# Row means of a 64 MB tensor: rows regrouped into three parts, one load ahead of the opening barrier

## Chip, cores, metric

One core of one Trainium2 chip. The metric is device time in microseconds (us) of one execution. "Ratio" is the figure that the measuring program gives for one kernel's fast runs against the other's in the same rounds, so it is not quite the ratio of the medians quoted beside it, nor of the plain means; the bracket after it is a 95% interval. "Step" or "pitch" is the distance in memory between the places where two neighbouring partitions begin to read.

## The reference

```python
x = np.random.randn(32, 512, 1024).astype(np.float32)     # 64 MiB
def reference(x, divisor):                                  # divisor = 1024.0
    return (np.sum(x, axis=-1) / divisor).astype(np.float32)
```

That is 16,384 rows of 4 KiB, 128 rows for each of the 128 partitions.

## The kernel before

It gives each partition 120 consecutive rows in a main part and 8 in a last part. Loads of 14 rows per partition go through three buffers. VectorE sums most rows, ScalarE a few of the later ones. The last row of each partition comes in three pieces and is closed by one accumulating operation, so that little is left to do after the last byte arrives.

```python
L = 8
M = J - L                                   # J = 128
x_main = bass.AP(tensor=x.tensor, offset=0, ap=[[M * D, P], [D, M], [1, D]])
x_last = bass.AP(tensor=x.tensor, offset=P * M * D, ap=[[L * D, P], [D, L], [1, D]])
# ... o_main, o_last likewise
main = [(14, 0)] * 6 + [(14, 4), (14, 6), (8, 4)]     # (rows, of them on ScalarE)
last = [(4, 2), (2, 1)]
# ... pools: bulk (3 buffers), one, psum
res = one.tile([P, M], F32, name="res")
fin = one.tile([P, L], F32, name="fin")               # q, r: the same size

for rows, on_act in main:
    t = bulk.tile([P, 14, D], F32, name="t")
    load(t[:, :rows, :], x_main[:, j : j + rows, :])
    sums(res[:, j : j + rows], t, rows, on_act)       # reduce_sum on VectorE, activation on ScalarE
    j += rows
# ... last: t4, t2 in tiles of their own; then one row, then three pieces pa, pb, pc of the last row
nc.gpsimd.tensor_scalar_mul(out=res, in0=res, scalar1=scale)
tc.keep_in_program_order(nc.sync.dma_start(out=o_main, in_=res))
# ... sums of pa, pb into two columns behind pc; means of the other last rows
nc.vector.tensor_scalar(
    out=scaled, in0=pc, scalar1=scale, scalar2=0.0, op0=MULT, op1=ADD, accum_out=fin[:, L - 1 :]
)
tc.keep_in_program_order(nc.sync.dma_start(out=o_last, in_=fin))
```

After the build, `start_loads_at_once` moves every load that waits for nothing (three of them) ahead of the opening barrier of all engines.

## Time and profile before

| | before |
|---|---|
| time, median of the first three runs | 161.70 us (161.69 to 161.78) |
| span in the profile | 160.1 us |
| VectorE / ScalarE busy | 75% / 13% |
| DMA engines under packets | 97.8% of the span |
| first load landed, first reduction starts | 19.58 us |

The page reads as a stream of loads with sums hidden behind it; the prediction shows the lines. Two lines of the DMA view complete them (columns: transfer, queue, operation, number, KB each, median us from issue to landing). They tell how deep the queue is: the last piece of the last row waits 35.7 us behind other loads, the store of 120 means 5.2 us.

```profile
pc<-in_x_dram SPq DMA_DIRECT2D x1, 160.0 KB, 35.7
...
out_dram<-res SPq DMA_DIRECT2D x1, 60.0 KB, 5.2
```

### The profile page before, as it was taken

To read this page: it belongs to the slowest core of one execution; us is meant where nothing else is said; L and a number is where in the kernel's file an instruction comes from. 1 tells how busy PE (TensorE), PEld (TensorE's weight loads), DVE (VectorE), ACT (ScalarE), POOL (GpSimd) and SP (SyncE) were. 2 spreads that over 40 slices of the span, in tenths; PEclk is the share of its full clock that TensorE was granted. 3 is DMA by queue.
4 is the path that set the end of the run, shared out by engine and by line. 5 is a ranking of instruction groups with operands and counts; after the bars stand their busy time and mean duration, and the time that the engine had idled before them with its cause. 6 is when DMAs were issued, how large, how long until landed. Compare 5 with 4: busy or idle time off the path is not lost.

```text
span 160.1 us, 138 instructions
## 1 busy us (share of the span) xinstructions
DVE 119.9 (75%) x16; ACT 20.7 (13%) x39; POOL 0.8 (1%) x6
## 2 busy tenths in 40 slices
DVE  0000199968998699959995999599987990497985
ACT  3000000000000000000000000000007300491973
POOL 0000000000000000000000000000000000000010
DMA  8899999998899999998899999999799999999993
GB/s 301 387 458 458 458 458 458 458 430 358 358 458 458 458 458 458 458 458 387 358 401 458 458 458 458 458 458 430 315 401 458 458 458 458 393 393 405 415 402 104
DMA packets 2448, 67.18 MB, mean 419 GB/s; under 512 B 528, under 2 KB 912, under 8 KB 1040
## 3 DMA queue, kind: packets, MB, share of 16 engines
q1 hardware_dynamic: 2448, 67.18, 97.8%
HBM read 67.11 MB, written 0.07 MB: 419 GB/s over the span
## 4 chain that ended last, share of the span: by engine, by line
DMA 67%; DVE 29%; another core or an unknown queue 1%; SPq 1%; issue 0%; DVEq 0%
DMA t<-in_x_dram 45%; DVE res L153 28%; DMA row<-in_x_dram 22%; SPq L142 1%; DVE q L173 1%; DVE scaled L195 0%; DVE pc L190 0%; DVE fin L191 0%; DVEq L195 0%; DVEq L229 0%
## 5 line engine op out<-in xcount | busy, mean ns | idle before, releaser
L153 DVE TENSOR_REDUCE res<-t 128x14 f32<-128x14336 f32 (+3 forms) x9 | 114.4, 12716 | 37.9 <-DMA t<-in_x_dram 37.9
L147 ACT ACTIVATE junk<-t 128x1024 f32<-128x1024 f32 x17 | 17.2, 1011 | 135.2 <-DMA t<-in_x_dram 135.2
L153 DVE TENSOR_REDUCE q<-t 128x2 f32<-128x2048 f32 (+1 forms) x2 | 3.5, 1752 | 0.7 <-DMA t<-in_x_dram 0.7
L147 ACT ACTIVATION_READ_ACCUMULATOR junk<-t 128x1 f32 x17 | 3.2, 186 | 0.0
L147 ACT ACT_TABLE_LOAD x1 | 1.3, 1283 | 1.7 <-PEq L215 1.7
L186 POOL TENSOR_SCALAR res<-res 128x120 f32<-128x120 f32 x1 | 0.5, 512 | 150.5 <-DVE res L153 150.5
L173 DVE TENSOR_REDUCE q<-row 128x1 f32<-128x768 f32 x1 | 1.0, 953 | 0.1
L195 DVE TENSOR_SCALAR_CACHE_REDUCE scaled<-pc 128x322 f32<-128x322 f32 x1 | 0.5, 490 | 0.1
L147 ACT ACTIVATE junk<-pa 128x448 f32<-128x448 f32 x1 | 0.5, 547 | 0.1
L190 DVE TENSOR_REDUCE pc<-pb 128x1 f32<-128x256 f32 x1 | 0.4, 412 | 0.0
L147 ACT ACTIVATE junk<-row 128x256 f32<-128x256 f32 x1 | 0.4, 387 | 0.1
L191 DVE SCALAR_TENSOR_TENSOR fin<-q,r 128x7 f32<-128x7 f32 x1 | 0.2, 167 | 0.0
L147 ACT ACTIVATION_READ_ACCUMULATOR junk<-row 128x1 f32 x1 | 0.2, 187 | 0.0
L147 ACT ACTIVATION_READ_ACCUMULATOR junk<-pa 128x1 f32 x1 | 0.2, 186 | 0.0
L139 POOL MEMSET r<- 128x8 f32 x1 | 0.1, 104 | 1.3 <-POOLq L215 1.3
L215 POOL MEMSET const-bfloat16-1.0<- 128x1 bf16 x1 | 0.1, 101 | 0.0
L215 POOL MEMSET const-uint8-127<- 128x1 uint8 x1 | 0.1, 101 | 0.0
L215 POOL MEMSET const-float32-0.0<- 128x1 f32 x1 | 0.1, 99 | 0.2 <-issue 0.2
L215 POOL MEMSET const-float32-1.0<- 128x1 f32 x1 | 0.1, 98 | 0.0
L195 DVE DVE_READ_ACCUMULATOR scaled<-pc 128x1 f32 x1 | 0.1, 82 | 0.0
## 6 DMA issues: line engine op xcount, KB each, us to landing
t<-in_x_dram SPq DMA_DIRECT2D x8, 7168.0 KB, 35.7
t<-in_x_dram SPq DMA_DIRECT2D x1, 4096.0 KB, 28.5
t<-in_x_dram SPq DMA_DIRECT2D x1, 2048.0 KB, 33.0
t<-in_x_dram SPq DMA_DIRECT2D x1, 1024.0 KB, 35.0
row<-in_x_dram SPq DMA_DIRECT2D x1, 512.0 KB, 35.8
pa<-in_x_dram SPq DMA_DIRECT2D x1, 224.0 KB, 36.0
pc<-in_x_dram SPq DMA_DIRECT2D x1, 160.0 KB, 35.7
pb<-in_x_dram SPq DMA_DIRECT2D x1, 128.0 KB, 35.9
```

The lines of the kernel that those rows point to most:

```text
L139: nc.gpsimd.memset(r, 0.0)
L142: tc.keep_in_program_order(nc.sync.dma_start(out=dst, in_=src))
L147: nc.scalar.activation(junk[:, :n], src, COPY, scale=by, accum_out=dst)
L153: nc.vector.reduce_sum(out=dst[:, :d], in_=t[:, :d, :], axis=AX)
L173: nc.vector.reduce_sum(out=q[:, j : j + 1], in_=row[:, :c], axis=AX)
L186: nc.gpsimd.tensor_scalar_mul(out=res, in0=res, scalar1=scale)
L190: nc.vector.reduce_sum(out=pc[:, D - b + 1 :], in_=pb, axis=AX)
L191: nc.vector.scalar_tensor_tensor(out=fin[:, : L - 1], in0=q[:, : L - 1], scalar=scale, in1=r[:, : L - 1], op0=MULT, op1=ADD)
L195: nc.vector.tensor_scalar(out=scaled, in0=pc, scalar1=scale, scalar2=0.0, op0=MULT, op1=ADD, accum_out=fin[:, L - 1 :])
L215: nc = _bacc.Bacc("TRN2", target_bir_lowering=False, num_devices=1)
```

## The change

Its intent: write back a first half of the means while loads still run, keep less ahead of the barrier, and leave 16 instead of 8 rows to the last part, whose very last row is closed by the same accumulating step. Cut to its core:

```diff
-def start_loads_at_once(nc):            # moves all loads that wait for nothing
+def start_first_load_at_once(nc):       # moves the first load alone
...
-    L = 8
-    M = J - L
-    x_main = bass.AP(tensor=x.tensor, offset=0, ap=[[M * D, P], [D, M], [1, D]])
-    x_last = bass.AP(tensor=x.tensor, offset=P * M * D, ap=[[L * D, P], [D, L], [1, D]])
+    B, L = 56, 16
+    def part(t, first, n, width):
+        cols = [[width, n], [1, width]] if width > 1 else [[1, n]]
+        return bass.AP(tensor=t.tensor, offset=first * P * width, ap=[[n * width, P]] + cols)
+    x_part = [part(x, 0, B, D), part(x, B, B, D), part(x, 2 * B, L, D)]
...
-    main = [(14, 0)] * 6 + [(14, 4), (14, 6), (8, 4)]
-    last = [(4, 2), (2, 1)]
+    main = [[(14, 0)] * 4, [(14, 0)] * 2 + [(14, 4), (14, 6)]]
+    last = [(8, 4), (4, 2), (2, 1)]     # the load of 8 uses a bulk buffer
-    res = one.tile([P, M], F32, name="res")
+    res = [one.tile([P, B], F32, name=f"res{k}") for k in range(2)]
...
+    def means_out(k):
+        nc.gpsimd.tensor_scalar_mul(out=res[k], in0=res[k], scalar1=scale)
+        tc.keep_in_program_order(nc.sync.dma_start(out=o_part[k], in_=res[k]))
...
+            if k == 1 and j == B:       # right after the eighth bulk load is issued
+                means_out(0)
...                                      # means_out(1) where the one store of means was
```

More of the change, by code (lines that the diff above doesn't have):

```diff
@@ L15 @@
 SP = mybir.EngineType.SP
-def start_loads_at_once(nc):
+def start_first_load_at_once(nc):
     first, body = nc.main_func.blocks[0], nc.main_func.blocks[1]
-    loads = []
-    for i in body.instructions:
-        if i.engine == SP:
-            if type(i).__name__ != "InstDMACopy" or (i.sync_info and i.sync_info.on_wait):
-                break
-            loads.append(i)
-    names = {i.name for i in loads}
-    assert names
-    body.instructions = [i for i in body.instructions if i.name not in names]
+    load = next(i for i in body.instructions if i.engine == SP)
+    assert type(load).__name__ == "InstDMACopy" and not load.sync_info.on_wait
+    body.instructions = [i for i in body.instructions if i.name != load.name]
     at = next(
@@ L34, in start_loads_at_once @@
     )
-    first.instructions = first.instructions[:at] + loads + first.instructions[at:]
+    first.instructions = first.instructions[:at] + [load] + first.instructions[at:]
 def with_sync(i, on_wait=None, on_update=None):
@@ L108 @@
     landed = nc.alloc_semaphore("landed")
-    nc.at_finalize(start_loads_at_once)
+    nc.at_finalize(start_first_load_at_once)
     nc.at_finalize(latest_wait_first)
@@ L117 @@
     assert J * P == N
-    L = 8
-    M = J - L
-    x_main = bass.AP(tensor=x.tensor, offset=0, ap=[[M * D, P], [D, M], [1, D]])
-    x_last = bass.AP(tensor=x.tensor, offset=P * M * D, ap=[[L * D, P], [D, L], [1, D]])
-    o_main = bass.AP(tensor=out.tensor, offset=0, ap=[[M, P], [1, M]])
-    o_last = bass.AP(tensor=out.tensor, offset=P * M, ap=[[L, P], [1, L]])
-    main = [(14, 0)] * 6 + [(14, 4), (14, 6), (8, 4)]
-    last = [(4, 2), (2, 1)]
-    assert sum(n for n, _ in main) == M and sum(n for n, _ in last) == L - 2
+    B, L = 56, 16
+    assert 2 * B + L == J
+    def part(t, first, n, width):
+        cols = [[width, n], [1, width]] if width > 1 else [[1, n]]
+        return bass.AP(tensor=t.tensor, offset=first * P * width, ap=[[n * width, P]] + cols)
+    x_part = [part(x, 0, B, D), part(x, B, B, D), part(x, 2 * B, L, D)]
+    o_part = [part(out, 0, B, 1), part(out, B, B, 1), part(out, 2 * B, L, 1)]
+    main = [[(14, 0)] * 4, [(14, 0)] * 2 + [(14, 4), (14, 6)]]
+    last = [(8, 4), (4, 2), (2, 1)]
+    assert all(sum(n for n, _ in m) == B for m in main) and sum(n for n, _ in last) == L - 2
     bulk = ctx.enter_context(tc.tile_pool(name="bulk", bufs=3))
@@ L153, in sums @@
         nc.vector.reduce_sum(out=dst[:, :d], in_=t[:, :d, :], axis=AX)
-    j = 0
-    for rows, on_act in main:
-        t = bulk.tile([P, 14, D], F32, name="t")
-        load(t[:, :rows, :], x_main[:, j : j + rows, :])
-        sums(res[:, j : j + rows], t, rows, on_act)
-        j += rows
+    def means_out(k):
+        nc.gpsimd.tensor_scalar_mul(out=res[k], in0=res[k], scalar1=scale)
+        tc.keep_in_program_order(nc.sync.dma_start(out=o_part[k], in_=res[k]))
+    for k in range(2):
+        j = 0
+        for rows, on_act in main[k]:
+            t = bulk.tile([P, 14, D], F32, name="t")
+            load(t, x_part[k][:, j : j + rows, :])
+            sums(res[k][:, j : j + rows], t, rows, on_act)
+            j += rows
+            if k == 1 and j == B:
+                means_out(0)
     j = 0
     for rows, on_act in last:
-        t = one.tile([P, rows, D], F32, name=f"t{rows}")
-        load(t, x_last[:, j : j + rows, :])
+        if rows == 8:
+            t = bulk.tile([P, 14, D], F32, name="t")[:, :8, :]
+        else:
+            t = one.tile([P, rows, D], F32, name=f"t{rows}")
+        load(t, x_part[2][:, j : j + rows, :])
         sums(q[:, j : j + rows], t, rows, on_act)
@@ L170 @@
     row = one.tile([P, D], F32, name="row")
-    load(row, x_last[:, j, :])
+    load(row, x_part[2][:, j, :])
     act_sum(r[:, j : j + 1], row[:, c:], by=scale)
@@ L180 @@
     pc = one.tile([P, D - b + 2], F32, name="pc")
-    load(pa, x_last[:, L - 1, :a])
-    load(pb, x_last[:, L - 1, a:b])
-    load(pc[:, : D - b], x_last[:, L - 1, b:])
-    nc.gpsimd.tensor_scalar_mul(out=res, in0=res, scalar1=scale)
-    tc.keep_in_program_order(nc.sync.dma_start(out=o_main, in_=res))
+    load(pa, x_part[2][:, L - 1, :a])
+    load(pb, x_part[2][:, L - 1, a:b])
+    load(pc[:, : D - b], x_part[2][:, L - 1, b:])
+    means_out(1)
     act_sum(pc[:, D - b : D - b + 1], pa)
@@ L197 @@
     )
-    tc.keep_in_program_order(nc.sync.dma_start(out=o_last, in_=fin))
+    tc.keep_in_program_order(nc.sync.dma_start(out=o_part[2], in_=fin))
 _INS = ['x', 'divisor']
```

## The prediction

> **What bounds the kernel now.** I looked first at the busy shares and the rows of slices on the profile page, then at the DMA section, then at the timeline for the cadence of the stages, and last at the chain of work that ended last for the tail.
>
> The page of the kernel before, its first lines, the DMA row of the slices and the queue line:
>
> ```profile
> span 160.1 us, 138 instructions
> ...
> DVE 119.9 (75%) x16; ACT 20.7 (13%) x39; POOL 0.8 (1%) x6
> ...
> DMA  8899999998899999998899999999799999999993
> ...
> q1 hardware_dynamic: 2448, 67.18, 97.8%
> HBM read 67.11 MB, written 0.07 MB: 419 GB/s over the span
> ```
>
> No compute engine is over 75%, while packets occupy the sixteen DMA engines for 97.8% of the span. The row shows no hole between the first two slices and the last. So this is a stream of loads with reductions hidden behind it. The timeline says the same with its cadence (columns: start, duration, engine, line, operation, and in brackets the idle time before it and what ended that):
>
> ```profile
> 19.58 15.09 DVE L153 TENSOR_REDUCE res<-t 128x14 f32<-128x14336 f32 x1 [19.58 <-DMA t<-in_x_dram]
> 36.52 15.09 DVE L153 TENSOR_REDUCE res<-t 128x14 f32<-128x14336 f32 x1 [1.86 <-DMA t<-in_x_dram]
> 53.47 15.09 DVE L153 TENSOR_REDUCE res<-t 128x14 f32<-128x14336 f32 x1 [1.86 <-DMA t<-in_x_dram]
> ```
>
> Each reduction takes 15.09 us, then VectorE idles 1.86 us for the next load. A load of 14 rows per partition is 128 x 57,344 bytes = 7.34 MB; one per 16.95 us is 433 GB/s. The trace's records of single packets agree: in steady state one engine moves 57,344 bytes in 2.116 us, 27.1 bytes per ns, and sixteen of them 433.6 GB/s. The slices of 315 or 358 GB/s on the page are not slow stretches: a slice is 4 us, a packet 2.1 us, and a packet's bytes fall into one slice. The packets themselves do not get longer there.
>
> Against this floor, 4.194 MB per engine at 27.1 bytes per ns are 154.8 us. The first packets start 1.02 us into the span and last 2.99 and 2.79 us on average in the first two groups of eight (steady state 2.12), about 0.8 us lost once. Small packets near the end cost some tenths more. That reaches the last load's last packet at 157.4 us. There is almost nothing left in the stream to win.
>
> The last stretch, from the chain of work that ended last (start, duration, what):
>
> ```profile
> 120.72 35.84 DMA row<-in_x_dram
> 156.56 0.02 issue
> 156.58 0.96 DVE q L173
> 157.55 0.02 issue
> 157.57 0.17 DVE fin L191
> 157.74 0.34 DVE pc L190
> 158.08 0.04 DVEq L195
> 158.11 0.07 issue
> 158.18 0.49 DVE scaled L195
> ```
>
> The load of the last but one row lands at 156.56 us; three VectorE operations follow back to back until 158.08; then the accumulating operation on the last row closes. The last piece of that row landed, by its semaphore, at 157.91 us, so it is about 0.15 us off the path. The final store is issued at 158.71 us. The tail follows the arrival of the loads, one to one.
>
> [...] The kernel before has a pitch of 480 KiB in its main part and 32 KiB in its last, both without loss here.[...]
>
> **The change part by part.** The instruction lists of the two kernels show the same eight loads of 14 rows, one of 8, of 4, of 2, of 1, and the three pieces of the last row, the same splits between VectorE and ScalarE, and the same three bulk buffers. Bytes read are the same.
>
> *Only the first load ahead of the barrier.* Loads two and three now come after the opening barrier, which before opened at 1.74 us (ACT table load and a memset start there); an issue is 0.4 us. Without two issues ahead of it the barrier should open near 0.9 to 1.0 us. The second load needs to be in the queue only when the first runs dry, near 18.5 us. It has some 17 us to spare, so this costs nothing. The first load leaves at the same place, so it gains nothing either. ScalarE and GpSimd start 0.8 us earlier and wait anyway.
>
> *The first 112 rows in two blocks of 56; the 8-row load joins the last part.* The pitch per partition goes from 480 KiB to 224 KiB, and for the last 16 rows to 64 KiB.[...] I put zero, with some risk, since no trace so far shows 224 or 64.
>
> *A store in the middle of the stream.* The first 56 means leave after the eighth bulk load has been issued (that is at VectorE's end of the fifth reduction, 87.36 + 15.09 = 102.45 us; the means were ready at 85.5 us). [...]its packets run between the last bulk load and the 8-row load, near 137.7 us, and everything behind moves by their length. Packets: 128 of 224 bytes, 8 per engine. Interpolating between the measured 32 bytes at 9 ns and 480 bytes at 26 ns gives 9 + 192/448 x 17 = 16 ns; eight are 0.13 us, with one more semaphore write (9 ns) 0.14 us. This is on the path: **+0.14 us**.
>
> *The second store* has 224 bytes instead of 480 and is issued after its reduction of 8 rows (about 147 us) rather than at 152.93. It still stands behind all loads, and ends 8 x 10 ns = 0.08 us sooner relative to them. Before, it landed at 158.13 us while the accumulating operation ran until 158.67, so its end was hidden: 0.
>
> *Waits of the queue.* There are eight completion semaphores in turn, and one more transfer shifts the turn: the last piece of the last row now waits for the eighth bulk load (138.2 us) instead of the seventh (121.2). Ahead of it are still the 8-row load and all the small ones, until about 157 us. Nothing runs dry: 0.
>
> *The tail.* The operation that makes the means of the last part has 15 columns instead of 7; at the reduction's 15,086 ns / 14,336 = 1.05 ns per column: **+0.01 us**, in the chain. The final store has 64 bytes a row instead of 32: 8 packets x about 1.2 ns = **+0.01 us**. The accumulating last operation is in both kernels, 322 columns wide.
>
> Sum: +0.14 + 0.01 + 0.01 = +0.16 us on 161.7, so 161.86; I round to 161.9.
>
> **The rivals.** *The new pitch slows the reads.* For it: 64 KiB is a power of two[...]; the last part's packets are short. Against it: a power of two (32 KiB) was used in the last part before, and its 16,384-byte packets ran at 26.6 bytes per ns against 27.1. If the last part lost 10% of its 20 us, that would be 163.9; if the main parts lost 1%, 163.2. I give something like this one chance in ten, most of it smaller.
>
> *The store in the stream makes a bubble.* A write to HBM between reads might let the DMA engines run dry[...]: the first packets of the program show about 0.8 us for starting cold. That would make 162.6. Against it: semaphore writes between loads cause no visible gap, and at the tail of before the store's packets follow the loads without one.
>
> *The opening gets faster.* Three issues in a row may have slowed the first packets; with one issue they may run at 2.1 us instead of 2.9. That would win at most 0.8 us: 161.0. Against it: all sixteen engines show the long first packet whatever its start (1.02 to 1.83 us)[...]. The opposite, the second load late, would need a barrier of over 15 us.
>
> **Range and chances.** Three timed runs of before lie within 0.09 us, so noise is small. From the opening I allow -0.3 us, from bubble and pitch +0.6: 161.5 to 162.5. Two per cent are 3.2 us. To be that much faster the stream would have to beat its wall of 154.8 us plus start and tail, which I cannot see: 0.01. To be that much slower the pitch would have to cost 2%: 0.02. Within 2%: 0.97.
>
> **What would show it right or wrong.** Right: a span near 160.3 us, DMA occupied 97 to 98%, VectorE's first reduction at 19.6 us and the following ones 16.95 apart with 1.86 us of idle time; ACT's table load near 0.9 us; the 8-row load landing near 148.0 instead of 147.87; the last piece of the last row with about 20 us from issue to landing instead of 35.7; the chain ending in the same operations. Wrong: reductions further apart than 16.95 us (pitch of the main parts), a later arrival of only the loads behind the store (bubble, if it is one step at 138 us; pitch of the last part, if it grows with each load), or a first reduction well before 19.5 us (opening). A VectorE that no longer idles between reductions would mean that I misread the bound altogether.

The sum of this forecast came to +0.16 us on 161.7, that is 161.86. Two things stand as estimates from packets of before: the wall of 154.8 us (27.1 bytes per ns in steady state) and the zero for the row blocks (27.1 at a pitch of 480 KiB, 26.6 at 32 KiB). That the store's packets keep their place among the loads, which the +0.14 us takes for granted, agrees with the trace of before: the packets of 57,344 bytes begin at 1.02 us, those of 32,768 at 137.17, of 16,384 at 146.87, and of the store of 480 bytes at 156.86 while loads run until 157.40, in the order of issue. The same trace has 16 semaphore updates for each of its 17 transfers, on eight semaphores in turn but for the last store, and 272 packets of 4 bytes of 9 ns, taken for their writes.

## The result, and the profile after

Changed: 161.91 us median of 4 runs (161.71 to 162.08). Before, in the same rounds: 161.69 (161.69 to 161.78). Ratio 1.0012 [0.9994, 1.0029]: no difference by 2%, nor one clear of zero. The time lies within 0.01 us of the rounded forecast, 161.9, and 0.05 us over its sum, 161.86.

The page of the changed kernel, the same four rows as before:

```profile
span 160.5 us, 140 instructions
...
DVE 119.9 (75%) x16; ACT 20.7 (13%) x39; POOL 1.0 (1%) x7
...
DMA  9899999999989999999888999999988999999991
...
q1 hardware_dynamic: 2592, 67.18, 97.5%
```

VectorE does the same work; there are 144 packets more (128 of the additional store, 16 of 4 bytes, the semaphore writes: 288 in the span for 18 transfers, 272 for 17 before) for the same bytes read. The timeline of the changed kernel (columns as in the prediction):

```profile
0.79 1.28 ACT L145 ACT_TABLE_LOAD   x1 [0.79 <-PEq L222]
...
20.06 15.09 DVE L151 TENSOR_REDUCE res<-t 128x14 f32<-128x14336 f32 x1 [20.06 <-DMA t<-in_x_dram]
36.98 15.09 DVE L151 TENSOR_REDUCE res<-t 128x14 f32<-128x14336 f32 x1 [1.83 <-DMA t<-in_x_dram]
53.92 15.09 DVE L151 TENSOR_REDUCE res<-t 128x14 f32<-128x14336 f32 x1 [1.86 <-DMA t<-in_x_dram]
```

The barrier opens at 0.79 us instead of 1.74, about as foreseen (0.9 to 1.0). The cadence is unchanged: 16.92 and 16.94 us. But the first reduction starts at 20.06 us, not at 19.58 as before, and that was not foreseen. The end of the chain of waits (start, duration, what):

```profile
155.69 1.22 DVE q L151
156.91 0.01 issue
156.93 0.96 DVE q L181
157.89 0.02 issue
157.91 0.17 DVE fin L198
...
158.53 0.49 DVE scaled L202
```

The same operations close, but the reduction of the last but one row starts only 0.35 us later than before (156.93 against 156.58), although the stream started 0.48 us later and a store stands in it. So something near the end got faster. The DMA view:

```profile
pc<-in_x_dram SPq DMA_DIRECT2D x1, 160.0 KB, 19.6
...
out_dram<-res SPq DMA_DIRECT2D x2, 28.0 KB, 23.0
```

The last piece is issued later (it waits for the eighth bulk load) and still lands in its turn; the median of the two stores, 23 us, is that of one in the middle of the queue and one at its end.

So the total was right, and the profile already says that its terms were not: a late start, a faster tail. The records of single packets say where. They do not name the engine, but sixteen packets run side by side (exactly sixteen in about 145 of the 150 us from 5 to 155 us, never fewer), which I take for one on each of the sixteen engines. The times at which these first sixteen packets of 57,344 bytes end:

```
                 first   second ...  15th    last of 16
before           3.86    3.92        4.35    4.38 us
changed          3.75    3.80        4.29    4.88 us
```

One engine alone is late by about half a microsecond, and it stays so: the last packet of the first load ends at 19.68 us, the one before it at 19.08, and the load counts as landed at 20.04 us (before: 19.17, 19.15 and 19.56). The loads that follow keep their distance of 16.9 us, so the late start stays in the whole stream: the last packet of the eight bulk loads ends at 138.15 us against 137.64 before. From 5 to 155 us the records show at least sixteen packets under way at every moment in the changed kernel, also around the store: nothing is lost in the stream itself.

### The profile page after: what moved, and what is told of

The parts are those of the page before. It is cut to its first block, busy times and chain, and to the rows that moved or that the text cites. A ratio compares the mean times of both kernels' runs of the same rounds, so it can differ in the third digit from the quotient of the medians.

```text
span 160.5 us, 140 instructions
## 1 busy us (share of the span) xinstructions
DVE 119.9 (75%) x16; ACT 20.7 (13%) x39; POOL 1.0 (1%) x7
## 4 chain that ended last, share of the span: by engine, by line
DMA 67%; DVE 30%; another core or an unknown queue 1%; SPq 0%; issue 0%; DVEq 0%
DMA t<-in_x_dram 67%; DVE res L151 28%; DVE q L151 1%; DVE q L181 1%; SPq L140 0%; DVE scaled L202 0%; DVE pc L197 0%; DVE fin L198 0%; DVEq L202 0%; DVEq L236 0%
## 5 line engine op out<-in xcount | busy, mean ns | idle before, releaser
L151 DVE TENSOR_REDUCE res<-t 128x14 f32<-128x14336 f32 (+2 forms) x8 | 110.0, 13753 | 37.3 <-DMA t<-in_x_dram 37.3
L151 DVE TENSOR_REDUCE q<-t 128x4 f32<-128x4096 f32 (+2 forms) x3 | 7.9, 2642 | 1.6 <-DMA t<-in_x_dram 1.5
L154 POOL TENSOR_SCALAR res<-res 128x56 f32<-128x56 f32 x2 | 0.7, 352 | 146.2 <-DVE res L151 146.2
## 6 DMA issues: line engine op xcount, KB each, us to landing
pc<-in_x_dram SPq DMA_DIRECT2D x1, 160.0 KB, 19.6
```

The costliest lines, as they stand in the source:

```text
L151: nc.vector.reduce_sum(out=dst[:, :d], in_=t[:, :d, :], axis=AX)
L154: nc.gpsimd.tensor_scalar_mul(out=res[k], in0=res[k], scalar1=scale)
```

## The experiments

Twelve runs, five rounds each, four to a chip. The timed figures of before on the three chips were 161.73, 161.69 and 161.76 us (nine runs each). For every run I also read two figures from its profile: the start of the first reduction ("first"), and the time of that same execution less this start ("rest"). The rest takes the chance of the start out of the comparison.

| kernel | step between partitions, first load | loads ahead | stores in mid-stream | median us | ratio to before | first us | rest us |
|---|---|---|---|---|---|---|---|
| before | 480 KiB | 3 | 0 | 161.69 | | 19.58 | 142.12 |
| changed | 224 | 1 | 1 | 161.91 | 1.0012 | 20.06 | 141.99 |
| r0 | 224 | 1 | 1 | 161.97 | 1.0015 | 19.82 | 141.99 |
| r1 | 480 | 1 | 0 | 161.80 | 1.0008 | 19.63 | 142.09 |
| r2 | 224 | 3 | 1 | 161.82 | 1.0010 | 19.94 | 141.98 |
| r3 | 448 | 3 | 0 | 161.35 | 0.9976 | 19.46 | 141.97 |
| r4 | 224 | 3 | 0 | 161.83 | 1.0009 | 20.09 | 141.91 |
| r5 | 224 | 3 | 2 | 162.15 | 1.0021 | 20.25 | 142.10 |
| r6 | 448 | 3 | 1 | 161.41 | 0.9985 | 19.23 | 142.01 |
| r7 | 448 | 1 | 0 | 161.37 | 0.9988 | 19.36 | 142.41 |
| r8 (= r3) | 448 | 3 | 0 | 161.37 | 0.9979 | 19.38 | 141.92 |
| r9 (= r7) | 448 | 1 | 0 | 161.49 | 0.9983 | 19.46 | 141.92 |
| r10 | 112 | 3 | 1 | 161.99 | 1.0017 | 19.82 | 142.17 |
| r11 | 336 | 3 | 1 | 162.16 | 1.0026 | 19.78 | 142.20 |

All results were correct. The steps are rows per partition in the first part times 4 KiB.

**r0: the changed kernel again.** No edit.

> The changed kernel again, as a control. Its four runs so far fell in two groups, 161.71 and 161.77 us, and 162.05 and 162.08, while before stayed within 0.09 us. Theory A (the opening): with a single load ahead of the barrier one DMA engine sometimes starts its first packet about 0.5 us late and stays late, so both groups appear again, near 161.75 and 162.05. Theory B (the mid-stream store and the layout decide): all runs near 161.85 and the two groups were chance of those executions.

161.97 us (161.81 to 162.24), ratio 1.0015 [1.0003, 1.0028]. The values are 161.81, 161.82, 161.97, 161.99, 162.24: a spread, not two groups. The kernel is slower than before by 0.15%, just clear of zero. The spread is 0.43 us, against 0.27 us in nine runs of before. The two groups of the first four runs did not come back, so nothing shows that they were more than chance.

**r1: before, with one load ahead of the barrier.**

```diff
-    nc.at_finalize(start_loads_at_once)
+    nc.at_finalize(start_first_load_at_once)
```

> The kernel before with only its first load ahead of the barrier, rows and stores as before. Theory A: runs spread from 161.7 to 162.1 us, median 0.1 to 0.3 over before, and a profile whose first landing is late by 0.5 us in some executions. Theory B: no different from before, 161.70 within 0.05, since the second load has 17 us to spare.

161.80 us (161.65 to 162.07), ratio 1.0008 [0.9995, 1.0021]. The mean is 0.13 us over before and two runs lie above all nine of before, which is a little of what theory A says; but its profile starts at 19.63 us and shows no late engine (last first packet done at 4.48 us). Undecided here.

**r2: the changed kernel, with three loads ahead.** The edit of r1 reversed.

> The changed kernel with all three first loads ahead of the barrier as in before. Theory A: the spread goes away; store +0.14 us and the faster last packets (their summed time per engine was 10.03 us in the changed kernel, 10.19 in before) -0.15 leave it equal to before, 161.7 within 0.08. Theory B: 161.85 without the spread of r0.

161.82 us (161.74 to 162.12), ratio 1.0010 [0.9996, 1.0024]. The late engine is still there: first packets done at 4.28 us for fifteen engines and 4.76 for the last, first reduction at 19.94 us. So the opening does not make it, and theory A falls as the cause of the late start.

**r3: before, with 112 and 16 rows.** Only the split is moved.

```diff
-    L = 8
+    L = 16
-    main = [(14, 0)] * 6 + [(14, 4), (14, 6), (8, 4)]
-    last = [(4, 2), (2, 1)]
+    main = [(14, 0)] * 6 + [(14, 4), (14, 6)]
+    last = [(8, 4), (4, 2), (2, 1)]     # the load of 8 in a bulk buffer, as in the changed kernel
```

> The kernel before with only the split moved: 112 rows in one part and 16 in the last, one store of 112 means at the end, three loads ahead. It tells the layout from the store. If the pitch of 64 KiB is what makes the last packets faster (1,280-byte packets 55 ns instead of 61, 8,192-byte ones 309 instead of 314), their sum is 10.03 us per engine again and the time about 0.12 to 0.15 us under before, 161.55. If it was chance or came from the shifted waits, 161.7. If a 64 KiB pitch costs anything, over 161.8.

161.35 us (161.24 to 161.43), ratio 0.9976 [0.9964, 0.9989]: faster than expected, and faster than both kernels. The last packets have the short times of the changed kernel (1,280 bytes in 55 ns, 8,192 in 309), and the start is 0.12 us earlier than in before. I took the pitch of 64 KiB for proved at this point. Run r10 says otherwise, below.

**r4: r2 with both stores at the end.**

```diff
-            if k == 1 and j == B:
-                means_out(0)
...
+    means_out(0)
     means_out(1)
```

> r2 with the first store of means moved behind all loads: no store in the stream. In the three profiles with blocks of 56 rows the first load landed at 19.8 to 20.0 us, in the three with 112 or 120 rows at 19.4 to 19.6. Theory C (addresses): the 224 KiB step between partitions makes one DMA engine late by 0.4 us at the start, so the first landing stays at 19.8 to 20.0 and only the store's 0.14 us goes: 161.68 against 161.82 of r2. Theory D (the store makes up the difference of r2 to r3): 161.35 as r3. Theory E (opening chance): the first landing is near 19.5 here.

161.83 us (161.67 to 162.00), ratio 1.0009 [0.9996, 1.0022]. Theory D falls: without a store in the stream the kernel is nowhere near r3, and the first load is as late as ever (20.09 us). The saving of the store does not show in the times at all; in the profile the rest is 141.91 against 141.98 us of r2.

**r5: r2 with the mid-stream store doubled.**

```diff
                 means_out(0)
+                tc.keep_in_program_order(nc.sync.dma_start(out=o_part[1], in_=res[0]))
```

> r2 with the mid-stream store doubled: the same 56 means are also written to the second block's place, which the later store overwrites, so the result stays right. By the packets of 224 bytes (8 per engine at 16 ns and a semaphore write of 9 ns) one more store costs 0.14 us: 161.96.[...] If it is hidden, +0.

162.15 us (161.74 to 162.35), ratio 1.0021 [1.0007, 1.0035]: 0.2 us over what I expected, but the profiled execution also drew the latest start of all, 20.25 us. Its rest is 142.10. A cleaner reading is the landing of the 8-row load less that of the first load: 128.30, 128.30 and 128.29 us in r3, r8 and r4 (no store between), 128.37 in the changed kernel, r0 and r2 (one), 128.47 here (two). By these differences a store of 128 packets of 224 bytes costs 0.07 to 0.10 us. Neither a bubble nor nothing; less than the 0.14 of its eight packets and the semaphore write put end to end.

**r6: r2 with both blocks out of one part of 112 rows.** Same loads, buffers, stores and order; only the addresses in memory differ.

```diff
-    x_part = [part(x, 0, B, D), part(x, B, B, D), part(x, 2 * B, L, D)]
+    x_part = [part(x, 0, B, D, 2 * B), part(x, 0, B, D, 2 * B, B), part(x, 2 * B, L, D, L)]
```

(`part` gets the step as a fifth argument and the row to begin at as a sixth; the outputs likewise.)

> r2 with the same blocks, loads and stores, but both blocks taken from one part of 112 rows per partition (step of 448 KiB instead of 224). Theory C: the first landing is back at 19.4 to 19.6 us and the time is r3 plus the store, 161.35 + 0.14 = 161.49. Theory D: the step does nothing, 161.82 as r2.

161.41 us (161.24 to 161.60), ratio 0.9985 [0.9972, 0.9997]. This is the run that decides. The timeline of r2 and then of r6, the first two reductions:

```profile
19.94 15.09 DVE L157 TENSOR_REDUCE res<-t 128x14 f32<-128x14336 f32 x1 [19.94 <-DMA t<-in_x_dram]
36.85 15.09 DVE L157 TENSOR_REDUCE res<-t 128x14 f32<-128x14336 f32 x1 [1.82 <-DMA t<-in_x_dram]
```

```profile
19.23 15.09 DVE L157 TENSOR_REDUCE res<-t 128x14 f32<-128x14336 f32 x1 [19.23 <-DMA t<-in_x_dram]
36.17 15.09 DVE L157 TENSOR_REDUCE res<-t 128x14 f32<-128x14336 f32 x1 [1.85 <-DMA t<-in_x_dram]
```

Both run at 16.91 to 16.94 us a load; r6 merely begins 0.71 us earlier, and its last engine has done its first packet at 4.10 us instead of 4.76. The addresses of the first load make the late start, in these single profiles by 0.7 us, in the means of the timed runs by 0.42 us (each against before on its own chip). The comparison on one chip and in the same rounds is with r4, which has the small step and no store in the stream: 161.83 against 161.41 us. Theory C holds, theory D falls.

**r7: r3 with one load ahead.** The edit of r1 on r3.

> r3 with only the first load ahead of the barrier. It repeats the comparison of r1 with before and r0 with r2 (+0.11 and +0.08 us in the mean, both within their intervals). If the opening costs, 161.45 with a wider spread than r3's 0.19 us; if not, 161.35.

161.37 us (161.32 to 161.77), ratio 0.9988 [0.9976, 1.0001]. Median as r3, spread wider through one run of 161.77. That run was the profiled one, and its loss is not at the start (19.36 us) but in the load of the last but one row: 28 of its 128 packets of 4,096 bytes took over 200 ns, up to 464, against 159 usual. The same appears in r3 (20 packets) and r4 (22), with three loads ahead, so the opening is not its cause. I don't know what is.

**r8 and r9: r3 and r7 again, side by side.**

> r3 again, beside r9, as the better version and the reference for the opening: 161.35 us, 0.2% under before.

> r7 again. Three pairs so far put one load ahead of the barrier 0.08 to 0.19 us behind three in the mean, none clear by itself. If the opening costs, 0.1 to 0.2 us over r8; if it was chance, within 0.05.

r8: 161.37 us (161.30 to 161.65), ratio 0.9979 [0.9967, 0.9992]; r9: 161.49 (161.38 to 161.60), ratio 0.9983 [0.9971, 0.9996]. The better version holds. For the opening there are now four pairs, one load ahead less three ahead, in the means: r1 +0.13, r0 less r2 +0.08, r7 less r3 +0.19 (each taken against before of its chip), r9 less r8 +0.06. All positive, none clear alone, and no profile shows where it would arise. A cost of about 0.1 us is likely and not shown.

**r10 and r11: blocks of 28, 84 and 16 rows, and of 84, 28 and 16.**

```diff
-    B, L = 56, 16
+    B, L = (28, 84), 16        # r11: (84, 28); loads and their split as in r2
```

> r2 with blocks of 28, 84 and 16 rows: the first load's partitions stand 112 KiB apart. In five profiles a step of 224 KiB let one DMA engine finish its first packet at 4.65 to 5.07 us where the others were done by 4.3, and with 448 or 480 KiB the last finished by 4.1 to 4.5. If the step of the first load is what matters and small steps are worse, the first landing is at 19.8 us or later and the time 161.8 or more. If 224 is special, near 19.4 us and 161.5.

> r2 with blocks of 84, 28 and 16 rows: the first six loads at a step of 336 KiB, the next two at 112 KiB. If only the first load's step matters and long steps are good, the first landing is at 19.4 us and the time 161.5 (r3 and the store). If a step of 112 KiB in the middle of the stream costs, the reductions behind it come later than 16.95 us after one another and the time is over 161.6.

r10: 161.99 us (161.90 to 162.19), ratio 1.0017 [1.0005, 1.0030]; r11: 162.16 (161.97 to 162.30), ratio 1.0026 [1.0012, 1.0039]. Both start late (19.82 and 19.78 us; one engine done with its first packet at 4.65 and 4.60 us, the others by 4.33 and 4.17). My simple reading of r11, that a long step is good, misses: 336 KiB is as late as 112 and 224. A step of 112 KiB in mid-stream costs no cadence (the reductions of r11 that follow are 16.95 and 16.96 us apart). Over all fourteen profiles the picture is without overlap: 112, 224 and 336 KiB give 19.78 to 20.25 us, 448 and 480 give 19.23 to 19.63. Why is open.

These two runs also overturned my account of the tail. Their last 16 rows come from the very addresses of r2 and r3, yet their packets have the long times of before. Mean duration of one packet, in ns:

```
bytes      16384   8192   4096   1792   1024   1280   sum per engine
before     614.9   313.6  161.3  75.2   46.9   61.1   10,185
changed    611.2   309.0  159.0  74.0   46.0   55.0   10,034
r10        613.5   313.3  162.3  75.0   46.5   60.3   10,167
```

Packets of 1,280 bytes took 59.9 to 61.1 ns in before, r1, r10 and r11, and 55.0 in the other ten of the fourteen profiles. The source step by itself is thus not the cause: it is 64 KiB in r10 and in r2. What the cause is was not shown. The traces hold no addresses, and no run moved the place where these loads land by itself.

## Why the prediction was right, and where not

The number was right. Three of its terms were wrong in size, and their errors partly cancelled.

- **The bound.** Right. The first seven loads follow one another by 16.91 to 16.95 us in every kernel, with VectorE idle 1.8 to 1.9 us before each; in before and in the changed kernel at least sixteen packets are under way from 5 to 155 us. No change of order or layout moved the rate, and so nothing came near 2%.
- **The store in the stream, +0.14 us.** Right in kind, too large: its packets of 224 bytes took exactly the interpolated 16 ns (by division 14 bytes per ns, against 18 at 480 bytes, 22 in loads of 1,024 and 27.1 in long packets), but the load behind it came only 0.07 to 0.10 us later (r4, r2, r5 with 0, 1 and 2 stores). The step that failed is adding packets end to end.
- **The row blocks, "I put zero, with some risk".** This is the step that was wrong. A step of 224 KiB costs about 0.4 us against one of 448 (r2 against r6), through one engine's late first packet. Against the 480 KiB of before it costs less, about 0.3 us by an estimate: r2 and r4 are 0.17 and 0.15 us over before in the means although their tail is 0.17 us shorter (next point), and r2 carries the store. The slow tails of r10 and r11 agree: 0.28 and 0.38 us over before, with the store. I had looked for this risk in the rate of the stream, where it is not: packets of 57,344 bytes took 2.116 us in steady state at 224 KiB as at 480. It is in the first packets, the last of which ended at 4.6 to 5.1 us with steps of 112, 224 and 336 KiB and at 4.1 to 4.5 with 448 and 480. Without the faster tail, which hid it, the time would have been near 162.1 (161.91 + 0.17).
- **The tail, +0.01 and +0.01.** The two terms are as forecast (15 columns took 175 ns instead of 167; a packet of the final store 10.5 ns instead of 8.6). But the packets of the last loads got 0.15 us per engine shorter, which I had not in the sum at all. The rest of before and r1 is 142.12 and 142.09 us, that of r3, r8 and r9, without a store in the stream too, 141.97, 141.92 and 141.92: about 0.17 us gained.
- **The opening, 0.** Nothing gained, as said: the first packet leaves at 1.02 us in both, and the second load is far from late (issued at 0.79 us in the changed kernel, where the first runs until 19.68). A loss of about 0.1 us is possible from four pairs and not shown.
- **The shifted waits of the queue and the second store, 0.** Right: the last piece lands in its turn 19.6 us after its issue, and the chain ends in the same operations.
- **The signs.** Two of those listed as right did not come: the first reduction at 19.6 us (20.06) and the 8-row load at 148.0 (148.40). None of those listed as wrong pointed to the error, since a start that is late by itself was not among them. The noise was also taken too small, 0.09 us from three runs; nine runs of before spread over up to 0.27 us.

Through means of timed runs, each against before of its chip: r3 -0.38 us, then the store and split of r6 to -0.25, the addresses of r2 to +0.17, one load ahead of r0 to +0.26 us. (The first step joins the tail with a better start: r3, r8, r9 begin at 19.38 to 19.46 us, before at 19.58.) The forecast of +0.16 us stood beside +0.22 of the medians by luck of two errors of opposite sign, -0.17 for the tail and about +0.3 for the step, with the store 0.06 us cheaper than thought; the range of 1 us was wide enough for all.

Of the rivals, "a bubble" falls by r5 (0.07 to 0.10 us a store, where the rival supposed about 0.8), "the opening gets faster" by r1 and r9, and "the new pitch slows the reads" was right about the cause and wrong about the place.

The version that the experiments point to is r3, the kernel before with 112 and 16 rows: 161.35 and 161.37 us in two sets, 0.2% under before and about 0.35% under the changed kernel.

## What to carry to other kernels

When a kernel sits on the DMA rate, read the first packets and the last ones. In mid-stream no run here won anything, and one engine that was late at the start was paid for at the end. Take the start out of a comparison (time less the start of the first consumer) before attributing tenths of a microsecond: two profiles of the same changed kernel began 0.24 us apart (20.06 and 19.82), more than the store or the tail is worth. And a forecast that hits can still be wrong by its terms: check each of them against the trace, and distrust a cause that fits until a run has tested it, as r10 did with the step of the last rows.
